# Feed-forward of a two-layer trunk: raw weights in three places in turn, and the read-back of turned products used later

## The chip, the cores and the metric

The kernel runs on one core of one Trainium2 chip. The metric is the device time of one execution in microseconds; the time of a version is the median over runs. One more execution was recorded by the hardware profiler, and every row below is from that one.

## The reference

Two layers over 256 tokens of width 2048 in float32. Each layer is a mixer, a gated feed-forward and a gated addition; the change is in the feed-forward:

```
FFN_HIDDEN = -(-8 * D_MODEL // (3 * 256)) * 256        # 5632

def _swiglu(h, norm_g, w_gate, w_up, w_down):
    xn = _rmsnorm(h, norm_g)
    return (jax.nn.silu(xn @ w_gate) * (xn @ w_up)) @ w_down
...
    for i in range(DEPTH):
...
            h = h + _odd_mixer(h, odd_norm[j], odd_w_in[j], odd_w_out[j])
        h = h + _swiglu(h, ffn_norm[i], ffn_w_gate[i], ffn_w_up[i], ffn_w_down[i])
        gate = jax.nn.sigmoid(_rmsnorm(h, ple_norm[i]) @ ple_w_gate[i])
        h = h + (p[i] @ ple_w_proj[i]) * gate
```

## The kernel before

Every float32 product is made of three TensorE products: the operand is split into a rounded part and the rest, and high x high, high x low and low x high are summed in PSUM. Weights go through a fixed pipe. SyncE issues the transfer of a raw tile (`raw`, four k tiles of 128 rows by 512 columns, 1 MB, 8 KB in each partition); ScalarE rounds two k tiles of it at a time into `whi` (line 106); VectorE subtracts to get `wlo` (line 107); TensorE multiplies (lines 226 to 228). There are two places for `raw` and four each for `whi` and `wlo`. A place of `raw` is free again when VectorE has read the last of it; the next transfer into it waits for that.

In this text a **unit** is the work on one raw tile, and a **half unit** the work on two of its k tiles; `tick` counts half units. Work that is not weights (norms, transposes, splits of activations) is put into a queue by `later` and runs, one piece per half unit, when its count has come.

The feed-forward (`ffn`) has 11 column blocks of 512 hidden columns in four groups of 3, 3, 3 and 2. A block makes gate and up products for both token tiles (`gate_up`). The first block of a layer does it plainly (`gate_up_8`). The other ten (`gate_up_7`) do six of the sixteen k tiles by seven products in place of eight: `pair` loads two k tiles of both weights into one raw tile, VectorE makes four sums of them (`work`, lines 849 to 851), and four pieces are split and multiplied (line 840). Three pairs alternate with plain units (`classical`); after the third pair VectorE combines banks (lines 885 to 888), the gate half is finished (line 893, Silu at line 897), then the up half (line 893 again, and line 921 for the product with Silu, kept in `sl`). So a block of this kind is 183 matmuls: 3 pairs of 21, and 10 k tiles x 2 token tiles x 2 weights x 3.

The hidden products must be turned so that hidden columns lie on partitions. `cross` does it: VectorE transposes 32x32 squares (`tq`, line 143), GpSimd issues four transfers to DRAM (`ty`, line 147) and two back (`tx`, line 151). `split_hid` then rounds `tx` into `hH` on ScalarE and makes `hL` on VectorE (lines 911, 912). It was allowed to run four half units after `cross`.

From the second group on, each block is followed by the down products of the group before (`down`): one or two column blocks of 12 k tiles, 72 matmuls each. In a layer, blocks 1 to 3 follow each other with no down product between; of the next seven periods from one block's transpose to the next, four hold one down product and three hold two.

The four engines run their queues in order. What stands where in a queue is set when the program is built: a list scheduler takes the instructions in the order of the code and moves them by its own estimate of when each can start. The pool `fp` (two places per name) holds what belongs to the feed-forward alone: `hH`, `hL`, `sl`, `tq`, `tx`.

Of the kernel before, what the change touches and what calls it, by code (L numbers as in the profile page):

```python
# [9 lines left out]
F32 = mybir.dt.float32  # L10
# [6 lines left out]
P = 128  # L17
NT = 2
D = 2048
KC = D // P  # L20
NB = 512
# [6 lines left out]
def trunk_kernel(ctx: ExitStack, tc: tile.TileContext, x, p, even_norm, even_w_in, even_w_gk,  # L28
# [109 lines left out]
    def cross(src, pool):  # L138

        tq = pool.tile([P, 4, NT, 4, 32], F32, name="tq", bufs=1)
        nc.vector.transpose(tq.rearrange("p a t m r -> p t m a r"),  # L143
                            src.rearrange("p t (m a c) -> p t m a c", a=4, c=32))
        y = yp.tile([4, 32, 4, NT, P], F32, name="ty")
        for q in range(4):
            nc.gpsimd.dma_start(y[:, :, q].rearrange("a c t n -> c a (t n)"),  # L147
                                tq[32 * q:32 * q + 32].rearrange("c a t m r -> c a (t m r)"))
        x = pool.tile([P, NT, 4, 4, 32], F32, name="tx", bufs=1)
        for t in range(NT):  # L150
            nc.gpsimd.dma_start(x[:, t].rearrange("p q m r -> p q (m r)"),
                                y[:, :, :, t].rearrange("a c q n -> (a c) q n"))
        return x.rearrange("p t q m r -> p m (t q) r")
# [21 lines left out]
    KU = 4  # L175
# [17 lines left out]
    def tick():  # L193
        state["unit"] += 1
        if fill:
            _, at, after, _ = fill[0]
            if at <= state["unit"] and (after is None or done[after[0]] + after[1] <= state["unit"]):
                run_fill()

    def unit(ps, stat, k0, cols, first, last, nk=KU, kw0=None, step=KU, pre=None, begun=0):  # L200


        kw0 = k0 if kw0 is None else kw0
        raw = wp.tile([P, KU, NB], F32, name="raw", bufs=2)
        n = sum(w for _, _, w in cols)
        for j in range(0, nk, step):
            o = 0
            for wt, c0, w in cols:
                nc.sync.dma_start(raw[:, j:min(j + step, nk), o:o + w],
                                  wt[(kw0 + j) * P:(kw0 + min(j + step, nk)) * P, c0:c0 + w]  # L210
                                  .rearrange("(k q) n -> q k n", q=P))
                o += w
        for j in range(0, nk, 2):
            hi = wp.tile([P, 2, NB], F32R, name="whi")
            lo = wp.tile([P, 2, NB], F32R, name="wlo")
            split_sb(raw[:, j:j + 2, :n], hi[:, :, :n], lo[:, :, :n])
            if pre:
                pre(k0 + j + 2)
            for c in range(2):
                k = k0 + j + c  # L220
                for tt in range(NT):
                    sh = stat[0][:, k, tt * P:(tt + 1) * P]
                    sl = stat[1][:, k, tt * P:(tt + 1) * P]
                    st = first and tt >= begun and j + c == 0
                    en = last and j + c == nk - 1
                    nc.tensor.matmul(ps[tt][:, :n], sh, hi[:, c, :n], start=st, stop=False)  # L226
                    nc.tensor.matmul(ps[tt][:, :n], sh, lo[:, c, :n], start=False, stop=False)  # L227
                    nc.tensor.matmul(ps[tt][:, :n], sl, hi[:, c, :n], start=False, stop=en)  # L228
            tick()
# [588 lines left out]
    def ffn(i, xs, nkey, nx_fn, fp):  # L818
# [22 lines left out]

        def pair(j, b):

            raw = wp.tile([P, KU, NB], F32, name="raw", bufs=2).rearrange("p (r c) n -> p r c n", r=2)
            for c, w in enumerate((ffn_w_gate[i], ffn_w_up[i])):
                nc.sync.dma_start(raw[:, :, c], w[2 * j * P:(2 * j + 2) * P, b * NB:(b + 1) * NB]
                                  .rearrange("(k q) n -> q k n", q=P))
# [23 lines left out]
        def gate_up_7(b):  # L871
# [17 lines left out]
            for n in range(2):  # L889
                while rest and rest[0][0] == n:  # L890
                    classical(*rest.pop(0))
                e = E[:, 2 * n:2 * n + 2]
                nc.vector.tensor_tensor(e, bank[:, 2 * n:2 * n + 2], e, OP.add)  # L893
                if n == 0:
                    sl = fp.tile([P, NT, NB], F32, name="sl")
                    for tt in range(NT):
                        nc.scalar.activation(sl[:, tt], E[:, tt], AF.Silu, scale=rstd_of(nkey)[:, tt:tt + 1])
            return sl, [E[:, 2 + tt] for tt in range(NT)]

        def gate_up_8(b):  # L900
            pg = block(xs, [(ffn_w_gate[i], b * NB, NB)], key=nkey)
            rs = rstd_of(nkey)
            sl = fp.tile([P, NT, NB], F32, name="sl")
            for tt in range(NT):
                nc.scalar.activation(sl[:, tt], pg[tt], AF.Silu, scale=rs[:, tt:tt + 1])
            later(sums_of_operand, key=("sT", i))
            return sl, block(xs, [(ffn_w_up[i], b * NB, NB)])
# [6 lines left out]
        def gate_up(gi, n):  # L914
# [7 lines left out]
                                               op1=OP.mult)  # L922
            x = {}
            later(lambda: x.update(x=cross(sl, fp)), key=("xT", i, b))
            later(lambda: split_hid(hT[gi], x["x"], 4 * n), key=("hT", i, b), after=(("xT", i, b), 4))

        def down(gi, cb, nx):
            for b in groups[gi]:
# [4 lines left out]
            if nx:  # L933
                finish_cols(nx, cb)

        for gi, g in enumerate(groups):
            for n in range(len(g)):
                gate_up(gi, n)
                if gi:
                    for cb in range(4 * n // len(g), 4 * (n + 1) // len(g)):  # L940
                        down(gi - 1, cb, None)
        nx = nx_fn()
        for cb in range(4):
            down(len(groups) - 1, cb, nx)
        return nx


# [155 lines left out]
```

## Time and profile before

| What | Value |
|---|---|
| Median of 3 runs | 2575.06 us (2572.66 to 2577.43) |
| Profiled execution, its own time | 2571.11 us |
| Its span, first to last instruction | 2569.4 us |
| TensorE busy, share of the span | 2442.5 us, 95% |
| VectorE busy | 1731.8 us, 67% |
| ScalarE busy | 1254.2 us, 49% |
| Transfers, mean rate | 184 GB/s, 473.13 MB |
| Mean granted TensorE clock | 0.986 of full |

A matmul's end is modelled as the time at which its last result is out, so matmuls that follow each other overlap in the record, and a TensorE at 95% is not at its best rate. How far it is from it is seen by the distance of the starts of neighbouring matmuls. "Idle before, releaser" tells how long an engine had nothing to do before an instruction, and what ended that.

### The profile page before, as it was taken

The page shows a single profiled execution, that of the slowest core. Times are in us where ns is not written, and L with a number is a line of the kernel's source. Part 1 is how long each engine was busy: PE and PEld are TensorE (multiplying, and loading weights), DVE is VectorE, ACT ScalarE, POOL GpSimd, SP SyncE. Part 2 cuts the span into 40 slices and gives each one's busy share as a digit, 9 for nine tenths or more (in the row PEclk, how much of TensorE's full clock was granted, in tenths as well). Part 3 has the DMA queues.
Part 4 walks back from the last instruction along what each step waited for, and adds up shares of the span by engine and source line. Part 5 has one row for each costly group of instructions (what it writes and reads, how often), then busy time and mean ns, then how long its engine had stood idle before and what let it go on. Part 6 is the DMA issues. An engine that isn't in the chain of part 4 may idle for free.

```text
span 2569.4 us, 28134 instructions
## 1 busy us (share of the span) xinstructions
PE 2442.5 (95%) x10786; PEld 1971.1 (77%) x10786; DVE 1731.8 (67%) x2009; ACT 1254.2 (49%) x1560; POOL 105.4 (4%) x177
## 2 busy tenths in 40 slices
PE   8999999889999999999999999998899999999998
PEld 7887787667777777778888888876677777777787
DVE  4865456777767766765667666567777677676664
ACT  6644454444444444446545655554444444444464
POOL 0000001000000000000000000010000000000000
PEclk9999999999999999999999999999999999999999
DMA  6454455555555665564554545555566555655663
GB/s 209 148 164 147 168 189 180 172 180 184 194 203 197 197 202 183 176 225 167 195 182 163 165 163 180 182 180 174 185 197 197 203 185 190 207 188 182 208 227 130
DMA packets 240681, 473.13 MB, mean 184 GB/s; under 512 B 12849, under 2 KB 19729, under 8 KB 240418
## 3 DMA queue, kind: packets, MB, share of 16 engines
q1 hardware_dynamic: 232514, 447.07, 52.4%
q0 software_dynamic: 7744, 23.08, 2.7%
q8 instruction: 84, 1.38, 0.2%
q10 hardware_dynamic: 288, 1.18, 0.1%
q14 instruction: 51, 0.42, 0.0%
HBM read 457.66 MB, written 13.63 MB: 183 GB/s over the span
## 4 chain that ended last, share of the span: by engine, by line
PE 61%; DMA 13%; DVE 13%; ACT 6%; issue 6%; POOL 0%; ACTq 0%; SPq 0%; POOLq 0%; DVEq 0%
PE bank L227 19%; PE bank L228 19%; PE bank L226 19%; DVE wlo L107 7%; DMA raw<-in_ffn_w_up_dram 5%; ACT whi L106 4%; DMA raw<-in_ffn_w_gate_dram 4%; PE bank L840 2%; DVE work L849 1%; DVE work L850 1%; DVE work L851 1%; DMA raw<-in_ffn_w_down_dram 1%; DMA raw<-in_odd_w_in_dram 1%; PE bank L165 1%; DMA tx<-ty 1%
## 5 line engine op out<-in xcount | busy, mean ns | idle before, releaser
L107 DVE TENSOR_TENSOR wlo<-raw,whi 128x1024 fp32r<-128x1024 f32 (+2 forms) x848 | 982.2, 1173 | 620.6 <-ACT whi L106 618.0
L106 ACT CAST whi<-raw 128x1024 fp32r<-128x1024 f32 (+2 forms) x848 | 841.4, 1010 | 1003.2 <-PE bank L228 406.0
L226 PE MATMUL bank<-whi,aH 128*128 128x512 f32 (+2 forms) x2176 | 854.2, 396 | 43.3 <-ACT whi L106 43.3
L227 PE MATMUL bank<-wlo,aH 128*128 128x512 f32 (+2 forms) x2176 | 856.0, 393 | 14.2 <-DVE wlo L107 13.7
L228 PE MATMUL bank<-whi,aL 128*128 128x512 f32 (+2 forms) x2176 | 851.7, 392 | 0.0
L226 PEld LDWEIGHTS bank<-whi,aH 128*128 128x128 f32 x2176 | 412.2, 190 | 136.2 <-ACT whi L106 53.4
L227 PEld LDWEIGHTS bank<-wlo,aH 128*128 128x128 f32 x2176 | 415.2, 191 | 114.8 <-DVE wlo L107 32.5
L228 PEld LDWEIGHTS bank<-whi,aL 128*128 128x128 f32 x2176 | 414.5, 190 | 84.9 <-issue 1.0
L226 PE MATMUL bank<-whi,hH 128*128 128x512 f32 x704 | 278.9, 396 | 17.9 <-DVE work L893 15.1
L228 PE MATMUL bank<-whi,hL 128*128 128x512 f32 x704 | 276.1, 392 | 0.0
L227 PE MATMUL bank<-wlo,hH 128*128 128x512 f32 x704 | 275.5, 391 | 0.0
L106 ACT CAST whi<-work 128x1024 fp32r<-128x1024 f32 x120 | 126.1, 1051 | 163.3 <-DVE work L849 88.1
L840 PE MATMUL bank<-whi,sT 128*128 128x512 f32 x480 | 178.6, 406 | 23.5 <-ACT whi L106 23.4
L107 DVE TENSOR_TENSOR wlo<-work,whi 128x1024 fp32r<-128x1024 f32 x120 | 146.7, 1222 | 38.8 <-ACT whi L106 36.7
L226 PEld LDWEIGHTS bank<-whi,hH 128*128 128x128 f32 x704 | 132.6, 188 | 50.1 <-ACT whi L106 19.8
L228 PEld LDWEIGHTS bank<-whi,hL 128*128 128x128 f32 x704 | 132.5, 188 | 29.9
L227 PEld LDWEIGHTS bank<-wlo,hH 128*128 128x128 f32 x704 | 132.7, 188 | 28.1
L840 PEld LDWEIGHTS bank<-whi,sT 128*128 128x128 f32 x480 | 90.2, 191 | 56.8 <-ACT whi L106 40.8
L840 PE MATMUL bank<-wlo,sT 128*128 128x512 f32 x240 | 97.9, 408 | 12.2 <-DVE wlo L107 12.2
L147 POOL DMA_DIRECT2D ty<-tq x88 | 48.6, 561 | 1233.3 <-DVE tq L143 1080.7
L849 DVE TENSOR_TENSOR work<-raw 128x1024 f32<-128x1024 f32 x60 | 73.3, 1222 | 5.7 <-DMA raw<-in_ffn_w_up_dram 5.5
L840 PE MATMUL bank<-whi,aH 128*128 128x512 f32 x180 | 70.8, 399 | 0.2 <-ACT whi L106 0.2
(253 smaller groups left out, 1623.1 us busy)
## 6 DMA issues: line engine op xcount, KB each, us to landing
raw<-in_ffn_w_down_dram SPq DMA_DIRECT2D x88, 1024.0 KB, 5.1
raw<-in_ffn_w_gate_dram SPq DMA_DIRECT2D x48, 1024.0 KB, 5.5
raw<-in_ffn_w_up_dram SPq DMA_DIRECT2D x48, 1024.0 KB, 5.3
raw<-in_odd_w_in_dram SPq DMA_DIRECT2D x48, 1024.0 KB, 5.2
raw<-in_ffn_w_gate_dram SPq DMA_DIRECT2D x80, 512.0 KB, 3.9
raw<-in_ffn_w_up_dram SPq DMA_DIRECT2D x80, 512.0 KB, 4.8
raw<-in_even_w_in_dram SPq DMA_DIRECT2D x36, 1024.0 KB, 5.0
raw<-in_ple_w_gate_dram SPq DMA_DIRECT2D x28, 1024.0 KB, 5.1
```

The costliest lines, as they stand in the source:

```text
L106: nc.scalar.copy(hi, raw)
L107: nc.vector.tensor_tensor(lo, raw, hi.bitcast(F32), OP.subtract)
L147: nc.gpsimd.dma_start(y[:, :, q].rearrange("a c t n -> c a (t n)"), tq[32 * q:32 * q + 32].rearrange("c a t m r -> c a (t m r)"))
L165: nc.tensor.transpose(ps[:, c, tt, :], h[:, tt, k * P:(k + 1) * P], ident)
L226: nc.tensor.matmul(ps[tt][:, :n], sh, hi[:, c, :n], start=st, stop=False)
L227: nc.tensor.matmul(ps[tt][:, :n], sh, lo[:, c, :n], start=False, stop=False)
L228: nc.tensor.matmul(ps[tt][:, :n], sl, hi[:, c, :n], start=False, stop=en)
L840: nc.tensor.matmul(bank[:, p], a, b, start=first and m == 0, stop=last and m == 2)
L849: nc.vector.tensor_tensor(T[:, 0:2], raw[:, 0], raw[:, :, 1], OP.add)
L850: nc.vector.tensor_tensor(T[:, 2], T[:, 1], raw[:, 0, 0], OP.add)
L851: nc.vector.tensor_tensor(T[:, 3], T[:, 2], raw[:, 1, 0], OP.add)
```

## The change

Four edits. The read-back `tx` is used ten half units after `cross` in place of four. The read-back shares one place with `tq` (tag `tq`) and `sl` has one place in place of two; that makes room in the pool `fp` for one more raw tile, `raw3`. While a feed-forward is being written down, every third raw tile comes from `raw3`, so that raw tiles take three places in turn; outside of it there are two, as before. Memory in use stays the same.

```
-        x = pool.tile([P, NT, 4, 4, 32], F32, name="tx", bufs=1)
+        x = pool.tile([P, NT, 4, 4, 32], F32, name="tx", tag="tq", bufs=1)
...
+    third = {"pool": None, "n": 0}
+
+    def raw_tile():
+
+        third["n"] += 1
+        if third["pool"] and third["n"] % 3 == 0:
+            return third["pool"].tile([P, KU, NB], F32, name="raw3", bufs=1)
+        return wp.tile([P, KU, NB], F32, name="raw", bufs=2)
+
     def unit(ps, stat, k0, cols, first, last, nk=KU, kw0=None, step=KU, pre=None, begun=0):
...
-        raw = wp.tile([P, KU, NB], F32, name="raw", bufs=2)
+        raw = raw_tile()
...
-            raw = wp.tile([P, KU, NB], F32, name="raw", bufs=2).rearrange("p (r c) n -> p r c n", r=2)
+            raw = raw_tile().rearrange("p (r c) n -> p r c n", r=2)
...
-                    sl = fp.tile([P, NT, NB], F32, name="sl")
+                    sl = fp.tile([P, NT, NB], F32, name="sl", bufs=1)
...
-            later(lambda: split_hid(hT[gi], x["x"], 4 * n), key=("hT", i, b), after=(("xT", i, b), 4))
+            later(lambda: split_hid(hT[gi], x["x"], 4 * n), key=("hT", i, b), after=(("xT", i, b), 10))
...
+        third["pool"] = fp
         for gi, g in enumerate(groups):
...
             down(len(groups) - 1, cb, nx)
+        third["pool"] = None
```

No instruction is added or taken away; places and order change. Three places in the queues follow, all around the third block of layer 0. Line numbers of the changed kernel are nine higher from `unit` on.

SyncE, from the last two units of the up half of block 2 to the second unit of block 3. Before, every tile is called `raw` and two places alternate:

```order
L209 DMA raw_3909<-in_ffn_w_up_dram 128x4x512
L209 DMA raw_3943<-in_ffn_w_up_dram 128x2x512
L846 DMA raw_3966<-in_ffn_w_gate_dram 128x2x512
L846 DMA raw_3966<-in_ffn_w_up_dram 128x2x512
L209 DMA raw_4019<-in_ffn_w_gate_dram 128x4x512
L846 DMA raw_4053<-in_ffn_w_gate_dram 128x2x512
L846 DMA raw_4053<-in_ffn_w_up_dram 128x2x512
L209 DMA raw_4098<-in_ffn_w_gate_dram 128x4x512
```

The changed program, the same stretch:

```order
L218 DMA raw_3909<-in_ffn_w_up_dram 128x4x512
L218 DMA raw_3943<-in_ffn_w_up_dram 128x2x512
L855 DMA raw3_3966<-in_ffn_w_gate_dram 128x2x512
L855 DMA raw3_3966<-in_ffn_w_up_dram 128x2x512
L218 DMA raw_4019<-in_ffn_w_gate_dram 128x4x512
L855 DMA raw_4053<-in_ffn_w_gate_dram 128x2x512
L855 DMA raw_4053<-in_ffn_w_up_dram 128x2x512
L218 DMA raw3_4096<-in_ffn_w_gate_dram 128x4x512
```

The transfers stand in the same order; each waits for the unit three before it in place of two before it. At one place per layer a transfer moves: the first one into `raw3` of layer 0 now stands among the weights of the mixer's output projection, between their fifth and sixth transfer.

VectorE, from the end of block 2 (`wlo_3946` is its last weight piece) through the first pair of block 3, before:

```order
L107 TENSOR_TENSOR wlo_3946<-raw_3943,whi_3945 128x1024
L107 TENSOR_TENSOR wlo_3973<-raw_3966,whi_3972 128x512
L849 TENSOR_TENSOR work_3006<-raw_3966 128x1024
L850 TENSOR_TENSOR work_3006<-work_3006,raw_3966 128x512
L851 TENSOR_TENSOR work_3006<-work_3006,raw_3966 128x512
L107 TENSOR_TENSOR wlo_3980<-work_3006,whi_3979 128x1024
L107 TENSOR_TENSOR wlo_3990<-work_3006,whi_3989 128x1024
L893 TENSOR_TENSOR work_3006<-bank_72,work_3006 128x1024
L107 TENSOR_TENSOR wlo_4000<-raw_3966,whi_3999 128x1024
```

The changed program, the same stretch (line 902 is line 893 of before):

```order
L107 TENSOR_TENSOR wlo_3946<-raw_3943,whi_3945 128x1024
L858 TENSOR_TENSOR work_3006<-raw3_3966 128x1024
L107 TENSOR_TENSOR wlo_3973<-raw3_3966,whi_3972 128x512
L859 TENSOR_TENSOR work_3006<-work_3006,raw3_3966 128x512
L860 TENSOR_TENSOR work_3006<-work_3006,raw3_3966 128x512
L107 TENSOR_TENSOR wlo_3980<-work_3006,whi_3979 128x1024
L107 TENSOR_TENSOR wlo_3990<-work_3006,whi_3989 128x1024
L858 TENSOR_TENSOR work_3006<-raw_4053 128x1024
L902 TENSOR_TENSOR work_3006<-bank_72,work_3006 128x1024
L107 TENSOR_TENSOR wlo_4000<-raw3_3966,whi_3999 128x1024
```

A sum of the second pair's raw tile (`raw_4053`) now stands ahead of the bank read that ends block 2 and of the last piece of the first pair.

ScalarE in the third pair of block 3, before; `hH` is the rounding of the read-back of block 2:

```order
L106 CAST whi_4138<-raw_4132 128x512
L911 CAST hH_3007<-tx_4016 128x1024
L106 CAST whi_4145<-work_3006 128x1024
L884 COPY work_3006<-bank_72 128x512
L106 CAST whi_4155<-work_3006 128x1024
L106 CAST whi_4165<-raw_4132 128x1024
```

The changed program:

```order
L106 CAST whi_4136<-raw_4130 128x512
L106 CAST whi_4143<-work_3006 128x1024
L920 CAST hH_3007<-tx_4016 128x1024
L106 CAST whi_4153<-work_3006 128x1024
L106 CAST whi_4163<-raw_4130 128x1024
L893 COPY work_3006<-bank_72 128x512
```

In ScalarE's queue the rounding of the read-back has moved by one cast, and the copy of a bank by three.

## Rows read from the trace of the kernel before

**Rows 1.** The page's first line.

```profile
span 2569.4 us, 28134 instructions
```

**Rows 2.** Timeline of VectorE, line 143: start, duration; blocks 0, 3, 10 of each layer.

```profile
434.85 1.25 DVE L143 STREAM_TRANSPOSE tq<-sl 128x1024 f32<-128x1024 f32 x1
...
595.80 1.24 DVE L143 STREAM_TRANSPOSE tq<-sl 128x1024 f32<-128x1024 f32 x1
...
1103.36 1.24 DVE L143 STREAM_TRANSPOSE tq<-sl 128x1024 f32<-128x1024 f32 x1
...
1716.89 1.25 DVE L143 STREAM_TRANSPOSE tq<-sl 128x1024 f32<-128x1024 f32 x1
...
1875.34 1.23 DVE L143 STREAM_TRANSPOSE tq<-sl 128x1024 f32<-128x1024 f32 x1
...
2383.52 1.24 DVE L143 STREAM_TRANSPOSE tq<-sl 128x1024 f32<-128x1024 f32 x1
```

**Rows 3.** Timeline of TensorE: first and 27th of 27 matmuls in unbroken sequence.

```profile
799.52 0.39 PE L226 MATMUL bank<-whi,aH 128*128 128x512 f32 x1
...
805.42 0.39 PE L228 MATMUL bank<-whi,aL 128*128 128x512 f32 x1
```

**Rows 4.** Waits, whole span: who waited for whom, us in total, times, longest.

```profile
ACT whi L106 <- DMA raw<-in_ffn_w_up_dram: 170.5, 51, 6.6
ACT whi L106 <- DMA raw<-in_ffn_w_gate_dram: 141.6, 49, 5.6
ACT whi L106 <- DMA raw<-in_ffn_w_down_dram: 131.9, 55, 4.1
...
ACT hH L911 <- DMA tx<-ty: 17.2, 8, 4.6
...
PE bank L226 <- DVE work L893: 15.1, 10, 2.4
```

**Rows 5.** VectorE's groups by form, 434 to 1104 us: count, busy us, mean ns, idle before.

```profile
L107 DVE TENSOR_TENSOR wlo<-raw,whi 128x1024 fp32r<-128x1024 f32 x194 | 231.8, 1219 | 96.8 <-ACT whi L106 96.4
...
L849 DVE TENSOR_TENSOR work<-raw 128x1024 f32<-128x1024 f32 x29 | 35.4, 1221 | 2.2 <-DMA raw<-in_ffn_w_up_dram 2.1
...
L107 DVE TENSOR_TENSOR wlo<-raw,whi 128x512 fp32r<-128x512 f32 x29 | 20.1, 692 | 45.8 <-ACT whi L106 45.7
...
L850 DVE TENSOR_TENSOR work<-work,raw 128x512 f32<-128x512 f32 x29 | 20.0, 690 | 0.8
L921 DVE SCALAR_TENSOR_TENSOR sl<-work,rstd,sl 128x512 f32<-128x512 f32 x20 | 14.1, 745 | 0.0
L143 DVE STREAM_TRANSPOSE tq<-sl 128x1024 f32<-128x1024 f32 x11 | 13.6, 1239 | 0.0
...
L912 DVE TENSOR_TENSOR hL<-tx,hH 128x1024 fp32r<-128x1024 f32 x10 | 12.2, 1219 | 4.2 <-ACT hH L911 4.2
```

**Rows 6.** From issue to landing: the down weights' tile view, then the gate weights'.

```profile
DMA to landing us min/median/max: 5.0/5.1/7.4
DMA to landing us min/median/max: 3.7/4.5/8.6
```

**Rows 7.** Timeline after the third pair of block 5, layer 0 (706 to 709 us).

```profile
706.15 1.22 DVE L893 TENSOR_TENSOR work<-bank,work 128x1024 f32<-128x1024 f32 x1 [0.77 <-PE bank L228]
706.95 1.04 ACT L106 CAST whi<-raw 128x1024 fp32r<-128x1024 f32 x1 [5.24 <-DMA raw<-in_ffn_w_up_dram]
...
708.04 1.12 PE L226 MATMUL bank<-whi,aH 128*128 128x512 f32 x2 [1.94 <-ACT whi L106]
```

**Rows 8.** Timeline in the third pair of block 2, layer 0 (507 to 510 us).

```profile
507.83 1.04 ACT L911 CAST hH<-tx 128x1024 fp32r<-128x1024 f32 x1 [4.62 <-DMA tx<-ty]
...
509.88 0.95 PE L840 MATMUL bank<-whi,sT 128*128 128x512 f32 x2 [2.84 <-ACT whi L106]
```

**Rows 9.** Line 667 (first and last start), and SyncE's sixth output-projection transfer of layer 0.

```profile
L667 PE MATMUL bank<-ident,ov x16: 270/272/273, 251.6 to 307.3; 128*128 128x128 f32 x16
...
313.07 0.37 SPq L209 DMA_DIRECT2D raw<-in_even_w_out_dram  x1
```

More of the change, by code (lines that the diff above doesn't have):

```diff
@@ L902, in gate_up_8 @@
             rs = rstd_of(nkey)
-            sl = fp.tile([P, NT, NB], F32, name="sl")
+            sl = fp.tile([P, NT, NB], F32, name="sl", bufs=1)
             for tt in range(NT):
```

## The prediction

> **What bounds the kernel now.** I read the page's first line first [rows 1] and set the profiled execution beside the median: it took 2571.1 us for a span of 2569.4, the three timed runs have a median of 2575.1. So my sum is made against 2571.1, and I add 4 at the end.
>
> Next comes TensorE's pace where nothing disturbs it. In an unbroken sequence 26 steps take 805.42 - 799.52 = 5.90 us [rows 3], 0.2269 us a matmul. A block of 183 matmuls can't take less than 41.5 us of TensorE, a down product of 72 not less than 16.3.
>
> Then I let VectorE's transpose of each block serve as a clock, since it ends every block [rows 2]. From block 0 to block 3 there are three periods without a down product: 160.95 us in layer 0 and 158.45 in layer 1, a mean of 53.2 us a period against 41.5 of TensorE. From block 3 to block 10 there are seven periods with ten down products: 507.6 and 508.2 us, against 7 x 183 + 720 = 2001 matmuls, 454.0 us. In all the feed-forward takes 70.3 us (six short periods) plus 107.8 us (fourteen long ones) more than TensorE needs. These 178 us are the stake; the rest of the program is not touched.
>
> Who makes TensorE late? The chain of waits says it [rows 4]: ScalarE's rounding waits 170.5, 141.6 and 131.9 us for the transfers of up, gate and down weights, 155 times, and what follows waits for ScalarE. One case in close view [rows 7]: after a third pair VectorE waits for a bank (0.77 us) and reads it in 1.22; ScalarE has waited 5.24 us for a raw tile; TensorE stands 1.94 us, and its next two matmuls take 1.12 us where two at pace take 0.39 + 0.23.
>
> Why is the raw tile late? With two places, a transfer starts when VectorE has read the last of the raw tile two before, and must be there when the one between has been worked off. It needs 5.1 us to land [rows 6] and 1.04 to be rounded [rows 7]: 6.1 us. From VectorE's forms [rows 5] a block of its work is: three pairs of 1.22 + 0.69 + 0.69 + 0.69 + 3 x 1.22 = 6.96 each, 20.9; ten plain pieces of 1.22, 12.2; the combination of banks 4 x 0.69 + 2 x 1.22 = 5.2; twice 0.745; transpose and hL 2.5. Sum 42.2 us over eight raw tiles, 5.3 each, and a plain tile alone gives only 2.44. So 6.1 doesn't fit into one tile's work, and VectorE shows it as idle time behind ScalarE: 96.4 and 45.7 us in layer 0 [rows 5].
>
> **The third place.** Now a transfer has two tiles' work: 10.6 us on average, 6.96 + 2.44 = 9.4 for a pair and a plain tile. 6.1 fits, and so does the longest landing seen, 8.6 [rows 6] and 1.04, all but 0.2. Two plain tiles give only 4.9 of VectorE's work, but TensorE needs 48 matmuls, 10.9 us, for them, so there it is TensorE that is waited for. The raw waits should go. What is late next differs by stage.
>
> Short periods: VectorE's 42.2 us exceed TensorE's 41.5, so VectorE becomes the bound. It will still wait for banks, 0.77 us [rows 7] twice a block, 1.5; and for the read-back: I take half of the 4.62 us that ScalarE waited for it in block 2 [rows 8], 2.3, since its use moves by only one cast. 42.2 + 1.5 + 2.3 = 46.0; saved 53.2 - 46.0 = 7.2 a period, six of them: **43 us**.
>
> Long periods: VectorE adds three raw tiles of 2.44 a down product, 7.3 us beside 16.3 of TensorE, so TensorE is the bound. What stays above its pace: the waits of TensorE for the bank that line 893 must read, 15.1 us over the whole span [rows 4], which no edit touches; and at the ends of pairs two waits of 0.77 and one slow restart (1.12 less 0.62, 0.5), 2.0 us a period, 28 in all. 107.8 - 15.1 - 28 = 64.7: **65 us** saved. Bounds of the two terms: if nothing but VectorE's work, and nothing but the bank waits, were left, 66 and 93; how much of the 2.0 and 2.3 stays I can't read, as no row shows a VectorE that is not waiting for raw tiles.
>
> **The longer wait before the read-back is used.** Six half units more in the code, but in the queue the rounding `hH` moves by a cast, the bank copy by three. Before, ScalarE waited 17.2 us for read-backs, eight times in twenty-two [rows 4]; if all of it went I would have to add it, if the faster blocks made it early again it stays. I price the edit by itself at 0, with -17 to 0 as bounds if all else stood still; what it may cost in the faster block is in the 2.3.
>
> **One place for `sl`, a shared place for `tx` and `tq`.** The next block's Silu writes `sl` some ten half units after the transpose has read it, and the read-back's transfers already wait for the transfers out, which read `tq`; the next transpose stands behind `hL` on the same engine. Cost 0; the cover is most of a block, some 20 us.
>
> **SyncE.** The order is kept but for the first `raw3` of each layer. In layer 0 it stands ahead of the sixth transfer of the output projection, and waits until buffers of the mixer are free: its last TensorE reader starts at 307.3, the sixth transfer goes out at 313.07 anyway [rows 9]. Cost 0 with 5.8 us of cover; without it each us of delay would go to the projection's weights, once in a layer.
>
> **VectorE's order.** This is a place where the change can lose. The first sum of the second pair now stands ahead of the bank read that ends the block, which TensorE needs. From the release of the place that this raw tile takes (the last `wlo` of block 2) to that sum, VectorE has 1.22 + 3 x 0.69 + 2 x 1.22 = 5.7 us of work [rows 5]. At a landing of 5.1 the wait is 0; at 8.6 [rows 6] it is 2.9, for VectorE, and for TensorE behind it. Twenty such blocks: 0 to 57 us. I take 0, nearer the median of either view than the maximum.
>
> That choice has a rule against it. Two transfers will often be under way at once, beside the turned products', and the gate weights already show 4.5 at the median but 8.6 at most [rows 6]. The Trainium skill, "DMA: Bandwidth & Descriptors", section "Issuing engines are not separate DMA queues", says that transfers from all engines run on the same 16 DMA engines and interleave, so two in flight would slow each other. By it the term would be nearer 57 than 0; no run here has three places yet, so the trace shows neither.
>
> Sum: 43 + 65 = 108 us; 2571.1 - 108 = 2463, and with the 4 us, **2467 us**.
>
> **Rivals.**
> *Half comes back.* The landings stretch to 8.6 us when they overlap, and the early sum of the second pair waits 2.9 us in each of twenty blocks: 108 - 57 = 51 saved, 2571.1 - 51 + 4 = 2524. For it: the longest landings exist already, at two places. Against it: 1 MB in 5.1 us eight times a block is 41 us, still inside 42.2.
>
> *Nearly all comes.* 66 + 93 = 159 saved: 2571.1 - 159 + 4 = 2416. It needs pairs that end without waits, against [rows 7].
>
> *The change doesn't do what it says.* The raw waits lie under others: VectorE's bank waits or the transfers' own rate hold the same place, 2575. Against it: ScalarE waits for nothing else nearly as long on the feed-forward's weights [rows 4], and 5.24 us in [rows 7] leave TensorE standing.
>
> *Slower.* ScalarE works in order, and behind `hH` stand the roundings that feed TensorE. As blocks get shorter the read-back is used sooner after its issue, and its transfers now share with a third weight transfer. If it is late by 4.62 us [rows 8] and by the 8.6 - 4.5 = 4.1 that a landing can stretch [rows 6] at all twenty-two splits, ScalarE stands 22 x 8.7 = 191 us; against 108 that is 83 us slower, 2571.1 + 83 + 4 = 2658. It decides from 108 / 22 = 4.9 us a split. For it: TensorE did stand 2.84 us at such a wait, in a block that was 53 us long. Against it: only 8 of 22 splits waited at all, 2.2 us each on average [rows 4], and long periods have a down product in which VectorE and ScalarE have time.
>
> **How the numbers follow.** Forecast 0.58; half comes back 0.25; nearly all 0.05; no change 0.05; slower 0.07. The first two give the range: 2425 is the forecast with three quarters of the waits that I left in the long and short periods (28 + 23) taken away, 38 us, and 4 for the spread of runs; 2540 is the half case with the read-back's 17.2 us on top. Left out are nearly all, no change and slower, 0.17. A measurement of this kernel can tell about 0.2%, 5 us, from no change: faster 0.88, the same 0.05, slower 0.07.
>
> **What would show it.** ScalarE's three waits for feed-forward weights should fall from 444 us to under 100, and VectorE's idle time ahead of `wlo` in layer 0 with them. From block 0 to 3 a layer should take near 3 x 46 = 138 us, from 3 to 10 about 475. A read-back wait above 5 us, and many of them, or VectorE idle ahead of line 858 on a raw transfer, would speak for the rivals. The prediction is wrong if landings grow above 8.6 us in number, if VectorE's idle time stays and only its name changes, or if the short periods stay above 50 us.

## The result and the profile after

| | Median | Runs | Ratio to the kernel before |
|---|---|---|---|
| Before | 2575.64 us | 4 | 1 |
| Changed | 2458.57 us (2457.39 to 2459.87) | 4 | 0.9547 (95% interval 0.953 to 0.9563) |

The change makes the kernel 4.5% faster, 117 us. The forecast was 2467 us with a range from 2425 to 2540. The profiled execution of the changed kernel took 2457.39 us, its span is 2455.7. Its page begins so:

```profile
span 2455.7 us, 28118 instructions
```

The span is 113.7 us shorter than that of [rows 1]. Where those went is read from the same clock as in the prediction, VectorE's transposes of blocks 0, 3 and 10 of each layer (timeline of VectorE; start, duration), which answer to [rows 2]:

```profile
436.34 1.24 DVE L143 STREAM_TRANSPOSE tq<-sl 128x1024 f32<-128x1024 f32 x1
...
578.54 1.24 DVE L143 STREAM_TRANSPOSE tq<-sl 128x1024 f32<-128x1024 f32 x1
...
1042.77 1.25 DVE L143 STREAM_TRANSPOSE tq<-sl 128x1024 f32<-128x1024 f32 x1
...
1659.18 1.23 DVE L143 STREAM_TRANSPOSE tq<-sl 128x1024 f32<-128x1024 f32 x1
...
1803.12 1.24 DVE L143 STREAM_TRANSPOSE tq<-sl 128x1024 f32<-128x1024 f32 x1
...
2268.66 1.25 DVE L143 STREAM_TRANSPOSE tq<-sl 128x1024 f32<-128x1024 f32 x1
```

The three short periods take 142.2 and 143.9 us, 47.7 each in place of 53.2: 33 us saved in all (forecast 43). The seven long ones take 464.2 and 465.5 us in place of 507.6 and 508.2: 86 saved (forecast 65). 33 + 86 is 5 more than the span lost, since the stretches ahead of block 0, from block 10 to the next layer and behind the last transpose are 1.5, 2.9 and 1.1 us longer by this clock. It is the transpose that moved in its queue there, not the work: TensorE starts its first pair at 433.5 us, before at 433.7. TensorE's own starts are the steadier clock. From the first matmul of the first pair of block 1 to the first matmul of the first down product, both layers together, it took 315.1 us and takes 285.0; from there to the first down product behind block 10 it took 1015.6 and takes 931.8. That is 30 and 84 us saved.

The waits of the whole span (who waited for whom: us in total, times, longest) answer to [rows 4]:

```profile
ACT whi L106 <- DMA raw<-in_ffn_w_up_dram: 57.8, 17, 4.5
...
DVE work L858 <- DMA raw<-in_ffn_w_up_dram: 34.2, 26, 4.0
...
ACT whi L106 <- DMA raw<-in_ffn_w_down_dram: 30.5, 16, 2.9
...
ACT hH L920 <- DMA tx<-ty: 24.5, 5, 6.7
DVE hL L921 <- ACT hH L920: 20.6, 4, 6.0
...
PE bank L235 <- DVE work L902: 16.9, 12, 1.4
```

ScalarE's waits for feed-forward weights are 57.8 and 30.5 us, where they were 444; those for gate weights are gone from the view. Three things are left: VectorE's wait at the first sum of a pair (line 858; 5.5 us before), the read-back (fewer waits, longer ones), and the bank that ends a block, as before.

Part of the gain is TensorE's clock. In each of these stretches (window in us, its length, busy time of each engine and its instructions, then the granted clock `PEclk`, the DMA share and the rate) the kernel before had:

```profile
434.85:595.80 160.95, 140.84 (x554) 107.11 (x553) 119.67 (x121) 71.43 (x79) 11.30 (x18) 0.94 0.55 183
595.80:1103.36 507.56, 475.41 (x2009) 378.08 (x2008) 365.77 (x369) 227.31 (x242) 25.86 (x42) 0.98 0.58 193
```

The changed kernel has:

```profile
436.34:578.54 142.20, 131.12 (x553) 105.50 (x552) 116.02 (x120) 70.61 (x78) 11.29 (x18) 0.96 0.64 209
578.54:1042.77 464.23, 456.41 (x1998) 374.19 (x1997) 360.27 (x368) 229.06 (x242) 25.86 (x42) 1.00 0.63 210
```

At or right behind stops of TensorE the granted clock fell to 0.50, 1.2 GHz in place of 2.4, eighteen times in the six short and fourteen long periods before, 68 us in all; it falls four times now, 20 us, all in the short periods. There matmuls start 0.43 us apart in place of 0.227. Worked out from these steps, an estimate, the clock cost 32 us before and 9 now, so that 23 of the 119 us saved came by it, 18 of them in the long periods. The matmuls of [rows 7] stood in such a stretch:

```profile
708.17:711.59 3.42, 3.28 (x7) 2.10 (x8) 2.30 (x2) 2.76 (x4) 0.00 (x0) 0.50 0.34 132
```

At the place of [rows 7], the end of the gate half of block 5, ScalarE still waits for an up tile, but nobody waits for ScalarE. Here is the timeline of ScalarE and VectorE:

```profile
678.88 2.00 ACT L106 CAST whi<-raw 128x1024 fp32r<-128x1024 f32 x2 [3.24 <-DMA raw<-in_ffn_w_up_dram]
...
679.56 1.21 DVE L902 TENSOR_TENSOR work<-bank,work 128x1024 f32<-128x1024 f32 x1
```

And of TensorE in the same place, where before it stood 1.94 us and then ran two matmuls in 1.12:

```profile
678.93 0.39 PE L237 MATMUL bank<-whi,aL 128*128 128x512 f32 x1
679.16 0.39 PE L235 MATMUL bank<-whi,aH 128*128 128x512 f32 x1
...
683.69 0.39 PE L237 MATMUL bank<-whi,aL 128*128 128x512 f32 x1
```

From 678.93 to 683.69 every step is at pace: 21 steps of 0.2267 us. At the read-back of block 1, in a short period, it looks otherwise (timeline; compare [rows 8]):

```profile
504.14 1.04 ACT L920 CAST hH<-tx 128x1024 fp32r<-128x1024 f32 x1 [6.74 <-DMA tx<-ty]
...
505.22 1.23 DVE L921 TENSOR_TENSOR hL<-tx,hH 128x1024 fp32r<-128x1024 f32 x1 [5.96 <-ACT hH L920]
...
506.19 0.79 PE L849 MATMUL bank<-whi,sT 128*128 128x512 f32 x1 [3.74 <-ACT whi L106]
```

ScalarE stands 6.74 us for the read-back, VectorE 5.96 and TensorE 3.74 behind it, and the matmul that ends the stop takes 0.79 us in place of 0.39: from 504.92 to 511.75 us the granted clock is 0.50. Four of the twenty-two read-backs wait 4.65 to 6.74 us, all in the second and third short period of a layer. From issue to landing, the tile views of gate and down weights say (min, median, max; compare [rows 6]):

```profile
DMA to landing us min/median/max: 3.5/4.8/7.4
...
DMA to landing us min/median/max: 4.8/5.7/7.9
```

The longest landing of an up tile is 9.1 us, where it was 7.6. Of the 300 weight transfers of the feed-forward three took longer than 8.6 us; before, none did.

### The profile page after: what moved, and what is told of

It reads as the page before. It is cut to its first block, busy times and chain, and to the rows that moved or that the text cites. A ratio compares the mean times of both kernels' runs of the same rounds, so it can differ in the third digit from the quotient of the medians.

```text
span 2455.7 us, 28118 instructions
## 1 busy us (share of the span) xinstructions
PE 2394.8 (98%) x10786; PEld 1965.8 (80%) x10786; DVE 1718.6 (70%) x2009; ACT 1259.2 (51%) x1560; POOL 105.3 (4%) x177
## 4 chain that ended last, share of the span: by engine, by line
PE 80%; DVE 8%; DMA 7%; ACT 3%; issue 2%; POOL 0%; SPq 0%; DVEq 0%; POOLq 0%; ACTq 0%
PE bank L235 23%; PE bank L236 23%; PE bank L237 23%; PE bank L849 8%; DVE wlo L107 3%; DMA raw<-in_ffn_w_up_dram 3%; DMA tx<-ty 1%; DMA raw<-in_odd_w_in_dram 1%; DMA ty<-tq 1%; DVE work L902 1%; PE bank L165 1%; DVE kT L135 1%; ACT whi L106 1%; DVE sl L930 1%; DVE tq L143 0%
## 5 line engine op out<-in xcount | busy, mean ns | idle before, releaser
L236 PE MATMUL bank<-wlo,aH 128*128 128x512 f32 (+2 forms) x2176 | 843.1, 388 | 4.8 <-DVE wlo L107 4.5
L237 PE MATMUL bank<-whi,aL 128*128 128x512 f32 (+2 forms) x2176 | 842.2, 387 | 0.0
L236 PEld LDWEIGHTS bank<-wlo,aH 128*128 128x128 f32 x2176 | 409.7, 188 | 89.0 <-DVE wlo L107 8.8
L237 PEld LDWEIGHTS bank<-whi,aL 128*128 128x128 f32 x2176 | 409.1, 188 | 84.6 <-issue 1.0
L106 ACT CAST whi<-work 128x1024 fp32r<-128x1024 f32 x120 | 126.4, 1053 | 188.8 <-PE bank L237 126.3
L849 PE MATMUL bank<-whi,sT 128*128 128x512 f32 x480 | 171.1, 396 | 11.7 <-ACT whi L106 11.7
L858 DVE TENSOR_TENSOR work<-raw 128x1024 f32<-128x1024 f32 x60 | 73.3, 1222 | 34.6 <-DMA raw<-in_ffn_w_up_dram 34.2
L849 PE MATMUL bank<-wlo,aH 128*128 128x512 f32 x180 | 72.7, 404 | 7.0 <-DVE wlo L107 7.0
```

The source lines that it names most:

```text
L106: nc.scalar.copy(hi, raw)
L849: nc.tensor.matmul(bank[:, p], a, b, start=first and m == 0, stop=last and m == 2)
L858: nc.vector.tensor_tensor(T[:, 0:2], raw[:, 0], raw[:, :, 1], OP.add)
```

## The experiments

The kernel before was timed with each group of runs; its medians were 2572.6 to 2575.6 us. The table gives for every run the six short periods together, the mean of one, and the fourteen long ones, from the starts of the transposes in its own trace. A transpose can move in VectorE's queue while the work stays where it was, so the column "By TensorE" has the six short periods once more by TensorE's starts, as above.

| Run | Median us | Ratio (95% interval) | Short periods | One | By TensorE | Long periods |
|---|---|---|---|---|---|---|
| before | 2575.6 | 1 | 319.4 | 53.2 | 315.1 | 1015.7 |
| changed | 2458.6 | 0.9547 (0.953 to 0.9563) | 286.1 | 47.7 | 285.0 | 929.8 |
| third place only | 2460.3 | 0.9561 (0.9545 to 0.9577) | 287.6 | 47.9 | 285.4 | 932.4 |
| longer wait only | 2573.2 | 1.0003 (0.9993 to 1.0014) | 314.9 | 52.5 | 310.5 | 1020.4 |
| third place from block 4 | 2487.5 | 0.9683 (0.9659 to 0.9706) | 318.3 | 53.0 | 313.9 | 930.7 |
| read-back later | 2460.5 | 0.9571 (0.9557 to 0.9586) | 280.7 | 46.8 | 281.6 | 936.1 |
| banks | 2444.7 | 0.9506 (0.9489 to 0.9522) | 282.3 | 47.1 | 277.9 | 920.2 |
| less for VectorE | 2449.1 | 0.9521 (0.9507 to 0.9535) | 282.9 | 47.2 | 277.6 | 929.8 |
| sums in order | 2444.2 | 0.9496 (0.9481 to 0.9511) | 273.2 | 45.5 | 270.9 | 931.0 |
| four places | 2482.6 | 0.9652 (0.9637 to 0.9667) | 267.5 | 44.6 | 269.7 | 943.7 |
| sums, read-back later | 2442.0 | 0.9491 (0.9473 to 0.9509) | 274.3 | 45.7 | 272.0 | 927.7 |
| sums, banks | 2419.4 | 0.9404 (0.9389 to 0.942) | 270.5 | 45.1 | 264.8 | 912.3 |
| sums, banks, read-back later | 2419.9 | 0.9405 (0.939 to 0.942) | 274.3 | 45.7 | 268.9 | 910.3 |
| sums, read-back later, no transfers for it | 2440.4 | 0.948 (0.9463 to 0.9496) | 272.9 | 45.5 | 270.5 | 935.0 |

**Which of the edits it is.** The third place without the longer wait:

```
-  ... after=(("xT", i, b), 10))
+  ... after=(("xT", i, b), 4))
```

> The changed kernel with the read-back's use allowed four half units after the transpose, as before, in place of ten. Theory (the third place does it all, the longer wait is worth nothing because the rounding of the read-back stands within one cast of the same place in the queue): 2459 us, within 5 us of the changed kernel. Rival (the longer wait is part of the gain): the read-back waits of ScalarE grow from 24.5 us by a few us at many of the twenty-two blocks, and the time is 2475 us or more.

2460.3 us: the whole gain is there. And the longer wait without the third place, in the kernel before:

```
-  ... after=(("xT", i, b), 4))
+  ... after=(("xT", i, b), 10))
```

> The kernel before with the read-back's use allowed ten half units after the transpose in place of four, two places for raw tiles, and the old places of sl and tx. Theory: no change, 2575 us, within 5, and ScalarE's three waits for feed-forward weights stay near 444 us. Rival (the wait before the read-back's use is part of the gain): 2565 us or less.

2573.2 us, no change, with 178.9, 146.0 and 126.3 us of ScalarE's waits for up, gate and down weights (451 in all). So the longer wait does nothing, and the places do it all.

**Where it acts.** The third place is kept out of blocks 0 to 3:

```
-        third["pool"] = fp
         for gi, g in enumerate(groups):
             for n in range(len(g)):
+                third["pool"] = fp if 3 * gi + n > 3 else None
```

> The changed kernel with the third place used only from block 4 of each layer on; blocks 0 to 3, so the three short periods of each layer, have two places as before. Theory (the gain is local: it comes where transfers have two tiles' work in place of one, 30 us in the short periods by TensorE's clock and 84 after them): the short periods go back to 53 us each and the time is 2487 to 2497. Rival (the short periods lose what they lose for the read-back, whatever the places): 2470 or less.

2487.5 us, inside the theory's band. The short periods are back at 53.0 us and the long ones stay at 930.7: each stretch has its own gain, none is carried over. In blocks 0 to 3 of this run `sl` has one place and `tx` shares with `tq`, as in the changed kernel, with two raw places: the short periods stand where they stood before (53.2), so the shared places cost nothing there.

**What is left in the long periods.** The first down product behind each block takes the gate half's banks:

```
                 if gi:
+                    turns["mm"] = 0
                     for cb in range(4 * n // len(g), 4 * (n + 1) // len(g)):
```

> The changed kernel with the first down product behind each block put into the banks of the gate half, which are free early, in place of whatever pair of banks is next in turn. Theory: the waits of TensorE for the bank that ends a block (16.9 us, twelve times, 1.4 each) are what is left above TensorE's pace in the long periods, ten of them go, and the time falls by 10 to 16 us, to 2443 to 2449. Rival (the wait moves to the next user of a bank, the first pair of the next block): within 5 us of 2458.6.

2444.7 us, 14 less, as the theory had it. TensorE's wait for line 902 is gone from the waits. In the changed kernel TensorE waited there twelve times, 1.41 us each, always at the first matmul of the first down product behind a block; ten of them lie in the long periods (timeline of TensorE):

```profile
1040.43 0.47 PE L235 MATMUL bank<-whi,hH 128*128 128x512 f32 x1 [1.41 <-DVE work L902]
```

**What is left in the short periods.** Six runs went after the read-back, VectorE and the places. The first binds the rounding `hH` to a later place in ScalarE's queue:

```
-        nc.scalar.copy(hi, raw)
+        state["cast"] = nc.scalar.copy(hi, raw).ins
...
-            nc.scalar.copy(d[0], x)
+            with tc.issue_after(state["cast"]):
+                nc.scalar.copy(d[0], x)
```

> The changed kernel, with the rounding of the read-back bound to stand behind the last weight rounding that is written ahead of it in the code; in ScalarE's queue it then stands four casts later than in the changed kernel at the short periods. Theory: in the second and third short period of each layer it is the wait for the read-back (four waits of 4.65 to 6.74 us, 23.7 in all) that stops TensorE, so they go, and the time falls by 15 to 30 us, to 2430 to 2444. Rival (VectorE is the bound there, and its idle time behind the read-back only moves): under 6 us of change. Second rival (the later use holds up the next transpose or the down products in the long periods): 2465 or more.

2460.5 us: the first rival's result. The waits for the read-back are gone, all of them, and the short periods gained 0.9 us each by the transposes, 0.6 by TensorE; the long ones lost 4 to 6 us, for which no run gives the cause. In place of the waits stands this, ten us earlier in the same block (timeline of that run):

```profile
493.10 1.22 DVE L858 TENSOR_TENSOR work<-raw 128x1024 f32<-128x1024 f32 x1 [2.90 <-DMA raw<-in_ffn_w_up_dram]
...
495.51 0.80 PE L849 MATMUL bank<-wlo,sT 128*128 128x512 f32 x1 [2.43 <-DVE wlo L107]
```

The first sum of the second pair stands ahead of the last pieces of the first, its up half has not landed, VectorE stands 2.90 us and TensorE 2.43. It is the early sum that the prediction priced at 0. The next run binds it behind the pieces that are written ahead of it:

```
-        nc.vector.tensor_tensor(lo, raw, hi.bitcast(F32), OP.subtract)
+        state["lo"] = nc.vector.tensor_tensor(lo, raw, hi.bitcast(F32), OP.subtract).ins
...
-            nc.vector.tensor_tensor(T[:, 0:2], raw[:, 0], raw[:, :, 1], OP.add)
+            with tc.issue_after(state["lo"]):
+                nc.vector.tensor_tensor(T[:, 0:2], raw[:, 0], raw[:, :, 1], OP.add)
```

> The changed kernel with the first sum of each pair bound to stand in VectorE's queue behind the weight pieces that are written ahead of it, as it stood before the change, so that no sum of a raw tile still under way stands ahead of the bank read and the last pieces of the pair before. Theory (VectorE's waits for up weights at that sum, 34.2 us in 26 waits, 4.0 at most, stop TensorE in the short periods, where VectorE has no time to spare): they go, and 6 to 15 us come back, 2444 to 2453. Rival (they lie beside TensorE's work, as in the long periods): within 5 of 2459. Second rival (the sums then come too late for the roundings that need them): 2464 or more.

2444.2 us, 14 below the changed kernel, all in the short periods (13 us by the transposes; the long ones 1 longer). The waits of this run:

```profile
ACT hH L921 <- DMA tx<-ty: 24.5, 8, 5.7
...
PE bank L236 <- DVE wlo L107: 4.1, 5, 0.8
...
DVE work L859 <- DMA raw<-in_ffn_w_up_dram: 3.0, 2, 1.7
```

The sum's wait fell from 34.2 us to 3.0, the read-back's stayed at 24.5. Whether VectorE's amount of work is what bounds was asked by leaving out two of its sums:

```
             nc.vector.tensor_tensor(T[:, 0:2], raw[:, 0], raw[:, :, 1], OP.add)
-            nc.vector.tensor_tensor(T[:, 2], T[:, 1], raw[:, 0, 0], OP.add)
-            nc.vector.tensor_tensor(T[:, 3], T[:, 2], raw[:, 1, 0], OP.add)
```

(GpSimd sets the two sums that are left out to zero where the operand's sums are made.)

> The changed kernel with the second and third of the four sums of each pair left out (lines 859 and 860; the last two hidden sums are then zero, so the hidden products are others). It takes 2 x 0.69 us of VectorE's work from each of three pairs, 4.1 us a block. Theory (in the short periods VectorE's in-order work is what bounds, at 42.2 us and what it loses by waiting): the six short periods give back 3 to 4 us each, some 20 us, and the long ones nothing: 2436 to 2444. Rival (the short periods are held by landings and the read-back, whatever VectorE has to do): 2452 or more.

2449.1 us, between the two bands and nearer the rival's: 9.5 us by the medians, 3.2 in the short periods by the transposes and 7.4 by TensorE, for 25 us of work taken away there. So VectorE's amount of work is at most a part of what bounds the changed kernel. ScalarE's waits for the read-back (25.5 us) and VectorE's at the first sum (36.8) stayed in this run, so it doesn't show what the amount of work would cost without them.

Then the read-back was bound later with the sums in order, by both edits above; the wait in the code is nine half units in this run and the others that join the two, in place of ten:

> The kernel with the sums in order (2444 us), with the rounding of the read-back bound four casts later in ScalarE's queue. Binding the read-back alone took its waits away and gained nothing, while an early sum stopped VectorE 2.9 us and TensorE 2.6 behind it. Theory (two stops in a row in each short period: with one away, the other takes its time; with the sums in order, the read-back's 24.5 us of waits are what is left): 10 to 22 us come back, 2422 to 2434. Rival (the read-back costs nothing in itself; the short periods are held by something else, for example by the landings of the up weights): within 5 of 2444.

2442.0 us, the rival again. No read-back waits, and still the short periods take 45.7. TensorE's waits for pieces of plain tiles have grown:

```profile
PE bank L236 <- DVE wlo L107: 13.3, 11, 2.2
```

The timeline of this run, behind the third pair of block 2:

```profile
501.74 2.00 ACT L106 CAST whi<-raw 128x1024 fp32r<-128x1024 f32 x2
...
503.15 1.22 DVE L923 TENSOR_TENSOR hL<-tx,hH 128x1024 fp32r<-128x1024 f32 x1
...
505.49 1.22 DVE L903 TENSOR_TENSOR work<-bank,work 128x1024 f32<-128x1024 f32 x1
...
506.21 2.00 ACT L106 CAST whi<-raw 128x1024 fp32r<-128x1024 f32 x2 [2.48 <-DMA raw<-in_ffn_w_up_dram]
...
506.62 3.49 DVE L107 TENSOR_TENSOR wlo<-raw,whi 128x1024 fp32r<-128x1024 f32 x3
...
507.89 0.50 PE L236 MATMUL bank<-wlo,aH 128*128 128x512 f32 x1 [2.18 <-DVE wlo L107]
```

The second up tile lands late for ScalarE, 2.48 us, and TensorE stands 2.18 us. It looks as if the one were the cause of the other, and the next run asks whether the read-back's transfers hold the tile up. It takes them out:

```
-        y = yp.tile([4, 32, 4, NT, P], F32, name="ty")
-        ...
+        x = tq.rearrange("p a t m r -> p (a t m r)").rearrange("p (t q m r) -> p t q m r", t=NT, q=4, m=4)
```

> The kernel of the run with the sums in order and the read-back bound later (2442 us), without the transfers of the turned products to DRAM and back: the rounding reads the transpose's own tile, at the same place in ScalarE's queue (the hidden columns then stand on other partitions, so the down products are others). Every other queue holds the same instructions. Theory (the read-back costs twice: by the wait for it, and by the raw transfers that land late while its transfers run, up to 7.8 us for up weights in the short periods of that kernel): the longest landings of up weights fall to 6 us or less, the waits that stayed after the read-back was moved (DVE wlo behind a late up tile, some 5 us a layer) go, and 8 to 20 us come back: 2422 to 2434. Rival (the landings stretch because two or three raw transfers run at once, whatever the read-back does): within 5 of 2442, with landings as before.

2440.4 us, the rival once more; the longest landing of an up tile is 8.1 us (8.0 with the transfers). At the same place stands the same stop:

```profile
506.58 1.99 ACT L106 CAST whi<-raw 128x1024 fp32r<-128x1024 f32 x2 [2.55 <-DMA raw<-in_ffn_w_up_dram]
...
508.39 0.50 PE L229 MATMUL bank<-wlo,aH 128*128 128x512 f32 x1 [2.18 <-DVE wlo L107]
```

The traces of both runs answer it another way: TensorE doesn't wait for the second up tile at all. The piece that it waits for at 507.89 is the `wlo` that VectorE makes from 506.62, and that is one of the first up tile, which ScalarE rounded from 501.74 on without a wait. VectorE had no idle time from 499.69 us to there. It made `hL` of the read-back, combined the banks and read the gate half's bank (line 903), and only then this piece. With the sums in order and the read-back unbound, `hL` comes nine us earlier (499.07 us) and the same piece stands ahead of the bank read (timeline of VectorE in that run):

```profile
508.33 1.21 DVE L107 TENSOR_TENSOR wlo<-raw,whi 128x1024 fp32r<-128x1024 f32 x1
...
511.75 1.22 DVE L903 TENSOR_TENSOR work<-bank,work 128x1024 f32<-128x1024 f32 x1 [1.00 <-PE bank L237]
```

Binding `hH` later on ScalarE puts `hL` later on VectorE, ahead of a piece that TensorE needs. ScalarE's wait for the second up tile lies beside that: its rounding ends at 507.25 us, and TensorE, with 24 matmuls of the first up tile to do from 505.1, would not have needed it before 510.5.

The last of the six runs has four raw places:

```
-        if third["pool"] and third["n"] % 3 == 0:
-            return third["pool"].tile([P, KU, NB], F32, name="raw3", bufs=1)
+        if third["pool"] and third["n"] % 2 == 0:
+            return third["pool"].tile([P, KU, NB], F32, name="raw3", bufs=2)
...
-            hi = wp.tile([P, 2, NB], F32R, name="whi")
+            hi = wp.tile([P, 2, NB], F32R, name="whi", bufs=3)
```

(and `wlo` likewise, here and in `pair`).

> The changed kernel with four places for raw tiles in the feed-forward (two and two), for which whi and wlo have three places each in place of four. Theory (with three places a transfer has 10.6 us of work to hide 6.1 in; what is left is VectorE's work, the read-back and the banks): no gain, 2456 to 2466. Rival (raw tiles still come late in the short periods, 88 us of ScalarE's waits for up and down weights remain): 2450 or less.

2482.6 us as a whole, outside both bands. But the short periods are the shortest of all runs by the transposes, 44.6 us, and by TensorE they take 269.7 us, as with the sums in order (270.9), though here the sums are early and the read-back unbound; no wait of any engine for up, gate or down weights above 0.2 us is left in it. The wait for the read-back is this:

```profile
ACT hH L920 <- DMA tx<-ty: 26.2, 16, 3.0
```

It lost 14 us in the long periods and 20 between block 10 of layer 0 and block 0 of layer 1. There TensorE stands four times for 2.8 to 3.3 us in the mixer of layer 1, 12.0 us, and runs 17 us at a granted clock of 0.50 behind these stops. In the mixer there are two raw places as before and only `whi` and `wlo` have fewer, so this loss is that of the three places for the rounded pieces; within the feed-forward the two effects were not separated.

**The best version.** The sums in order and the banks together:

> The kernel with the sums in order (2444 us) and the first down product in the banks of the gate half. Theory (the two edits work in different stretches, the short periods and the long ones, and add up): 2428 to 2434, 14 below 2444. Rival (part of what the banks gave, 2 and 6 us of it, came in the short periods and is the same time as the sums'): 2434 to 2440.

2419.4 us, below both bands: 39 below the changed kernel, 11 more than the 28 of the two edits apart. The waits of TensorE tell why; with the banks alone:

```profile
PEld bank L849 <- DVE wlo L107: 24.0, 26, 2.7
PE bank L849 <- DVE wlo L107: 13.8, 19, 2.2
```

With both:

```profile
PEld bank L849 <- DVE wlo L107: 3.6, 10, 0.4
```

In the changed kernel these two rows were 16.1 and 10.2 us. Where the bank wait was taken away, TensorE came to the pairs earlier and waited there for pieces that the early sum had delayed; with the sum in order it doesn't. All of TensorE's waits in the long periods together say the same: 16.2 us in the changed kernel, 6.1 with the banks, 17.0 with the sums in order, none with both. With the read-back bound later as well:

> The changed kernel with the sums in order, the read-back bound four casts later and the first down product in the banks of the gate half. Theory: the three add up, 2408 to 2422. Rival (the read-back's later place gains nothing, or costs in the long periods what it gives in the short ones): 2426 or more.

2419.9 us, no different. The number lies in the theory's band, but only through the other two edits: the read-back adds nothing. TensorE's stops of 2.2 us behind `hL` are in this run too.

## Why the prediction was right, and where it was not

**The mechanism held.** A transfer with two tiles' work in place of one lands in time: ScalarE's waits for weights fell from 444 to 88 us (forecast: under 100), the longer wait gives nothing (third place only, longer wait only), the shared places cost nothing where that could be seen (third place from block 4), the first `raw3` stands ahead of the sixth output-projection transfer and doesn't delay it (312.94 us, before 313.07), and the gain is in the stretches named. 117 us came where 108 were forecast. That the sum came so close is in part luck: one term was 21 us too small and the other 10 too large.

**The long periods: 86 for 65.** The term mis-sized is the 28 us for the ends of pairs. Over TensorE's 2 x 454.0 the long periods still take 21.8 us, and ten bank waits of line 902, 14.1 us, are in them. So some 8 are left for all else. The 0.77 and the slow restart of [rows 7] were read in a place where a raw tile was late; with the tile on time, VectorE's wait for the bank lies beside TensorE's work. And the slow restart ran at half clock from 708.17 us on, which no term of the prediction names: the granted clock of the long periods rose from 0.98 to 1.00, and the restarts went with the stops.

**The short periods: 33 for 43.** Four steps were off. First, "VectorE becomes the bound": the 42.2 us are a sum of durations, and in the record neighbouring instructions of VectorE overlap, three pieces of 1.22 us taking 3.49 and not 3.66. VectorE is busy 116.0 us in three short periods of the changed kernel, 38.7 each, less than TensorE's 41.5; and with 4.1 us a block less to do, the short periods gave back 0.5 to 1.2 each. That 46.0 was forecast and 47.7 came is therefore luck: what fills the period is stops (TensorE stands 10.9 and 12.0 us in the three of each layer) and what follows them. Second, the 42.2 us were spread over eight raw tiles, by volume. A block takes nine, since each weight's last two k tiles take a whole place, so the mean work on a tile is 4.7 us and not 5.3. No stop of TensorE could be put down to this.

Third, the choice of 0 for the early sum: putting it in order gives 14 us, between the 0 taken and the 57 of the upper bound. The prediction took from the Trainium skill, "DMA: Bandwidth & Descriptors", section "Issuing engines are not separate DMA queues", that transfers interleave on the same engines, and that the term should then be nearer 57. The down tiles' median did rise from 5.1 to 5.7 us and the longest up landing to 9.1, but the sum waits 1.3 us on average (34.2 in 26), and in the long periods putting it in order gained nothing by itself. So two of the signs that the prediction had named for its rivals came, VectorE idle ahead of line 858 and three read-back waits above 5 us, at a small part of the rivals' price.

**The read-back.** This is the fourth step. The 2.3 us a period were too little as a wait (5.9 at the mean in the four waits of the second and third short periods) and too much as a price. With the wait gone, other stops take its time: the early sum in the changed kernel, and with the sums in order the piece behind `hL`, with or without the read-back's transfers. The slower case needed 4.9 us at each of twenty-two blocks; five waited.

**The offset.** The profiled execution after stands 1.2 us under its median, where I added 4 from before.

What stays open: the short periods at 45.7 us with the sums in order and the read-back late, 4.2 above TensorE's 41.5. In each layer two stops behind `hL` with their restarts take 4.9 us, the bank wait ahead of the first down product 1.7, and a stretch at half clock 1.6. That is 8 of the 12.6 us of three periods; the rest is spread over short waits. A run that moves `hH` and keeps `hL` behind the piece that TensorE needs was not made, and neither was one that joins four places to the sums in order, with room for all pieces. What makes the clock fall is not shown either, only that in the kernels before and after each fall in these stretches came at or right behind a stop.

## What to carry to other kernels

Count places for a streamed tile by the work on the tiles between: with n places a transfer has the work on n - 1 tiles to land in. Here 6.1 us fitted into the work on two tiles and not into that on one. A wait that the profile shows on the path is worth what the next late thing leaves of it: take it away alone, and look where the time went, before it is priced. When a transfer gets more lead, look at what an in-order queue now starts early for it; an operation that may wait belongs behind the ones that others wait for. An operation that is moved in one queue takes along what hangs on it in the next. And a wait of one engine beside a stop of another is not its cause until the instruction that ended the stop is traced back.

## Not expected

24.5 us of ScalarE's waits for the read-back could be taken away for no gain in the changed kernel, and for 2.3 us in the one with the sums in order. Two edits in different stretches gave 39 us together and 28 apart, since the wait at the bank had been a cover for VectorE's early sum. And the waits for weights cost more than the time that TensorE stood: behind the stops it ran at half clock, which an estimate puts at 32 us before and 9 after.
